# A fourth pair by seven products in eight groups of each feed-forward, with the joins, transposes and first loads re-ordered

## The chip, the core and the metric

The kernel runs on one core of a Trainium2 chip. The metric is the device time of one execution in microseconds (us), lower is better. Before the change it is 2086.14 us, the median of three runs (2083.84 to 2087.06). The core has a matrix engine (TensorE, PE in the profile, with its weight loads as PEld), a vector engine (VectorE, DVE), a scalar engine (ScalarE, ACT), GpSimd (POOL) and SyncE (SP), which issues most of the DMAs. Each engine executes its instructions in the order in which the program issues them. TensorE alone writes PSUM, the accumulator memory, in banks of 512 columns; everything else is in SBUF.

## What is computed

A Conformer block on x of 256 rows by 2048 features: a feed-forward, a mixer (convolution and gated units), cross-attention into a memory, a second feed-forward and a last norm. The change lies in the two feed-forwards:

```python
def swiglu_ffn(h, w_in, w_out):            # w_in 2048 x 11264, w_out 5632 x 2048
    gate, up = jnp.split(h @ w_in, 2, axis=-1)
    return (jax.nn.silu(gate) * up) @ w_out

h = rms_norm(x, ffn1_norm[l])
x = x + MACARON_SCALE * swiglu_ffn(h, ffn1_w_in[l], ffn1_w_out[l])
...
h = rms_norm(x, ffn2_norm[l])
x = x + MACARON_SCALE * swiglu_ffn(h, ffn2_w_in[l], ffn2_w_out[l])
```

All is float32. Each operand is split into a high part in the matrix engine's float32r format and the rest, and a product is three matmuls: high by high, high by low, low by high.

## The kernel before

**Groups.** A feed-forward takes the hidden width of 5632 in 11 groups of 512 (`NG`, counted from 0). A group multiplies 256 tokens by 1024 columns (512 of gate, 512 of up) over 2048 features, that is 16 weights of 128 x 1024. After the groups come two blocks of the second product, 44 weights each.

**Pairs.** Group 0 takes its 16 weights plainly: 12 matmuls of 512 columns for each (`by_two`, two token halves by two column halves by three, L358 to L361). In groups 1 to 10 the weights go in 8 pairs, by a pattern of letters. A pair with C is taken plainly, 24 matmuls. A pair with S is taken as a 2 x 2 product with seven products instead of eight (`seven`, L345 to L347): 21 matmuls, for which sums of weight halves (L628, L629, L632, L635) and sums of x (`sides`) are made first. The seven products stand in accumulators "5", "7", "6", "1" and, with the plain ones, in "2", "3", "4", "8". The pattern is `SCSCSCCC`: three pairs by seven.

**Joins.** After the second of the four items of a group's last pair by seven, "5", "7", "6" and "1" are complete: `joins_sevens` copies "1" (ScalarE, L694) and makes the common sums (VectorE, L695 to L698). After the group's last item `joins_eights` adds "2", "3", "4", "8" (L702), and `give` applies silu, scale and product (L712, L714) and transposes the group's result in 32 x 32 blocks on VectorE (L717, 128 x 1024). The result leaves to DRAM (`leaves`, SP) behind the third item of the next group; it comes back later (`back`) and `turn` splits it into the operand of the second product. Six accumulators come from one pool (`ps`) and two ("6", "7") from another (`pa`), so a group's banks become those of the next.

**A weight's way.** An item of the line (`Item`, `Line`) is a weight or a part of one: it is loaded by SP into one of eight raw buffers, ScalarE casts it to the high part (L451), VectorE subtracts (L428) and so makes the low part, TensorE uses it. `Line.produce` issues casts ahead of use as far as places for the parts are free (nine) and `most` allows; the subtraction of an item is issued after the cast of the next. In each group some weights are summed instead (`SUMMED`, by number 0 to 15): ScalarE writes the negated high part and the high part (L566, L567), and an accumulating DMA of GpSimd (L568) adds the weight from DRAM; VectorE does nothing for them. Two buffers (hl_s and half of `more`) serve these in turn; each is filled anew after its use. In the groups with three pairs by seven, weights 2, 7 and 13 are summed.

**Operands.** In a group x (`x_hl`) is the stationary operand and the weight's parts the moving one. The weight's places are three of `hl`, two of `ring`, two of `hl_l`, one of `hl_h` and one of `more`; in the second product also `hl_out` and `more_out`, with `hl_s`, `hA`, `hB`, `hC` as stationary operands.

**Where tiles lie.** Pools lie one behind the other in a partition in the order in which they are opened, and a tile takes a multiple of 32 bytes. By the laid-out program, tiles of `const`, `big`, `wraw`, `whl` and `ev` (x_hl, ring, hA, hB, more_out, raw, hl) start at a multiple of 64 bytes. The small tiles of `st` follow. What lies behind them, the pools `xt`, `own`, `low` and later ones (more, raws_out, hl_s, h, z, hl_out, sums, hl_l, hC), starts at 32 modulo 64. `hl_h` is laid from the upper end and starts at 32 modulo 64 too. A tile of 8 floats, `to_64` (L97), stands in `st` already.

**The start.** Group 0 of the first feed-forward loads x by columns (`xT`, two at a time) beside its weights, and x by rows in four quarters of 512 KB, whose squares (L894) give the root `r_x` that `give` needs. All are on SP's queue in the order of the weights: the quarters stand in front of weights 2, 4, 6 and 8, the squares behind weights 2, 4, 6 and 8.

Of the kernel before, what the change touches and what calls it, by code (L numbers as in the profile page):

```python
# [33 lines left out]
SCALE = float(HD) ** -0.5  # L34


PATTERNS = (["SCSCSCCC"] * 11, ["SCSCSCCC"] * 11)


SUMMED = tuple([()] + [(7, 13)] + [(2, 7, 13)] * 8 + [(2, 7)] for _ in range(2))  # L40

OUT_S = ((9, 11, 13, 15, 17, 19), (9, 11, 13, 15, 17, 19))
# [37 lines left out]
def layer(ctx: ExitStack, tc: tile.TileContext, a: dict):  # L82
# [299 lines left out]
    class Item:  # L382

        def __init__(self, use=None, loads=(), held=None, keys=(), pre=None, src=None, n=1024, frees=(), post=(), make=None):
            self.use, self.loads, self.held, self.keys, self.pre, self.src = use, loads, held, keys, pre, src
            self.n, self.frees, self.post, self.make = n, frees, list(post), make
            self.place = self.hl = None

    class Line:

# [73 lines left out]
        def run(self):  # L464
            traced = nc.cur_bb.bb.instructions
            begin = len(traced)
            self.fetch()
            self.produce()
            for s, item in enumerate(self.items):
                assert self.made > s, (s, len(self.places), len(self.raws), item.missing)  # L470
                if self.ahead is item:
                    self.subtract()
                if item.use is not None:
                    item.use(item.hl)
                if item.place is not None:
                    self.places.append(item.place)
                self.used = s + 1
                self.produce()
                for part in item.post:
                    part()  # L480
            last = {}
            for i in traced[begin:]:
                if i.engine in last:
                    tc.add_manual_dep(
                        i, last[i.engine].name,
                        mybir.DependencyInfo(mybir.DependencyClass.NoSync, mybir.DependencyReason.DATA),
                        reason="line",
                    )
                last[i.engine] = i

    class FeedForward:
# [6 lines left out]
        def __init__(self, stack, tags, name, x_hl, gain, w_in, w_out, patterns, sums, steps, out_s):  # L498
# [37 lines left out]
            self.in_spare = self.fixed(raws)  # L536
            self.line.places.extend(self.in_ring + self.in_low + self.in_high)
            self.line.raws.extend([Place(lambda: wraw.tile([P, 1024], F32, name="raw")) for _ in range(4)] + self.in_spare)

        def fixed(self, tiles):  # L540
            return [Place(lambda x=x: x) for x in tiles]
# [131 lines left out]
        def pairs(self, j, steps, kinds, b):  # L673
# [16 lines left out]
                    i += 1  # L690
            return out

        def joins_sevens(self, b, p1, u2, u4, u5):
            nc.scalar.copy(out=p1, in_=b["1"])  # L694
            nc.vector.tensor_tensor(out=u2, in0=p1, in1=b["6"], op=ALU.add)  # L695
            nc.vector.tensor_tensor(out=u4, in0=u2, in1=b["5"], op=ALU.add)
            nc.vector.tensor_tensor(out=u2, in0=u2, in1=b["7"], op=ALU.add)
            nc.vector.tensor_tensor(out=u5, in0=u2, in1=b["5"], op=ALU.add)  # L698

        def joins_eights(self, b, p1, u2, u4, u5):  # L700
            for acc, u in (("2", p1), ("3", u4), ("4", u2), ("8", u5)):
# [2 lines left out]
        def give(self, j, gates, ups):  # L704
            flat, r = self.stage[j % 2], self.r
            h = flat.rearrange("p (q t n) -> p q t n", q=4, t=2)

            def by_q(x):
                return x.rearrange("p (q n) -> p q n", q=4)

            for t in range(2):
                nc.scalar.activation(out=h[:, :, t], in_=by_q(gates[t]), func=AF.Silu, scale=r[:, t:t + 1])  # L712
            for t in range(2):
                nc.vector.scalar_tensor_tensor(  # L714
                    out=h[:, :, t], in0=by_q(ups[t]), scalar=r[:, t:t + 1], in1=h[:, :, t], op0=ALU.mult, op1=ALU.mult
                )
            nc.vector.transpose(out=flat, in_=flat)  # L717

        def leaves(self, j):
# [7 lines left out]

        def group(self, j):
            b = {"begun": set()}
            parts = self.pairs(j, range(len(self.patterns[j])), lambda p: self.patterns[j][p] == "S", b)  # L730
            p1, u2, u4, u5 = self.u
            self.last_seven[1].post.append(lambda: self.joins_sevens(b, p1, u2, u4, u5))
            parts[-1][-1].post += [
                lambda: self.joins_eights(b, p1, u2, u4, u5), lambda: self.give(j, (p1, u2), (u4, u5)),
            ]
            return parts

        def block(self, n, places, done):
            b = {"begun": set()}
            steps = self.steps[n]  # L740
            parts = self.pairs(NG + n, steps[0], lambda p: p in steps[1], b)
            made = []

            def join():
                made.append(places())
                self.joins_sevens(b, *made[0])

            self.last_seven[1].post.append(join)
            if done is not None:
                parts[-1][-1].post.append(lambda: (self.joins_eights(b, *made[0]), done(made[0])))  # L750
            return parts, b, made

        def begin(self, before, after, scales):
            acc = []

            def use(k):
                def go(w):
                    if k == 0:
                        acc.extend(token_accs())
                    first = [(t, g) for t in range(2) for g in range(2)] if k == 0 else []  # L760
                    by_two(acc, self.x_hl[:, k], w[:, 0], w[:, 1], k, first, k == KD - 1)
                return go

            items = []
            for k in range(KD):
                held = {}
                items.append(Item(
                    use(k), [(0, self.w_in[0, :, k], None)], held, src=lambda held=held: held[0][0], frees=(0,),
                    post=after.get(k, []),
                ))  # L770
                items[-1].pre = lambda k=k: before(k)
            for i in range(len(self.spairs)):
                for q, part in enumerate(self.sides(i)):
                    items[3 * i + q + 3].post.append(part)
            self.r, parts = scales
            parts = parts + [
                lambda: nc.scalar.activation(out=st.tile([P, 1], F32, name="warm"), in_=ones[:, 0:1], func=AF.Silu)
            ]
            for i, part in enumerate(parts):
                items[14 - len(parts) + i].post.append(part)  # L780
            items[13].post.append(lambda: self.summed_load(self.early))
            items[15].post += [
                lambda: self.give(0, [acc[t][0] for t in range(2)], [acc[t][1] for t in range(2)]),
                lambda: self.summed(self.early),
            ]
            self.ends = [KD]
            return items
# [71 lines left out]
    def groups(ff, items):  # L859


        for j in range(1, NG):
            parts = ff.group(j)
            flat = [item for part in parts for item in part]
            flat[2].post.append(lambda j=j: ff.leaves(j - 1))
            if j == 1:
                flat[4].post.append(lambda: ff.summed(1 - ff.early))
            if j == NG - 1:
                flat[1].post.append(lambda: (ff.back(0), ff.back(1)))
                flat[4].post.append(lambda: ff.back(2))  # L870
                for i, item in enumerate(flat[-6:]):
                    item.post.insert(0, ff.turn(i))
                ff.in_ring[0].until = ff.in_ring[1].until = len(items) + flat.index(ff.last_seven[-1])
            items += flat
# [5 lines left out]
    with ExitStack() as stack:  # L880
# [7 lines left out]
        def x_load(c):  # L888
            return lambda: nc.sync.dma_start(
                out=squares[c], in_=a["x"][c // 2 * P:(c // 2 + 1) * P, c % 2 * 1024:(c % 2 + 1) * 1024]  # L890
            )
# [10 lines left out]
        root[0] = both(  # L902
            lambda: nc.vector.tensor_tensor(out=r_x, in0=tot[:, 0], in1=tot[:, 1], op=ALU.add), root[0]
        )
        items = ff.begin(x_arrives, {2 * c + 2: [x_squares(c)] for c in range(4)}, (r_x, root))
        halves = [slice(G, 2 * G), slice(0, G)]

        def early_load():
# [8 lines left out]
        for k in range(1, KD):  # L917
            beside_load = []
            if k % 2 == 0:
                beside_load.append(lambda k=k: nc.sync.dma_start(out=xT[:, k:k + 2], in_=a["xT"][:, k:k + 2]))  # L920
            if k in (2, 4, 6, 8):
                beside_load.append(x_load(k // 2 - 1))
            if k == 11:
                beside_load.append(lambda: nc.sync.dma_start(out=pv, in_=a["pv"]))
            items[k].loads = [(0, a["ffn1_w_in"][0, :, k], both(*beside_load))]
# [43 lines left out]
        def more_out():  # L969
# [5 lines left out]
            ff.out_forms = [  # L975
                forms[:, q * 1024:(q + 1) * 1024].rearrange("p (f two n) -> p f two n", two=2, n=P) for q in range(6)
            ]
            ff.leaves(NG - 1)

        def hl_out():  # L980
            line.places.extend(ff.fixed([ff.own.tile([P, 2, 1024], F32R, name="hl_out", tag="z")]))
# [30 lines left out]
        flat = [item for part in parts for item in part]  # L1012
        for i in range(6, 2 * NG):
            flat[i - 6].post.append(ff.turn(i))
        flat[16].post.append(hl_out)
        items += flat
        ff.in_high[0].until = len(items) - 1
# [13 lines left out]
                flat.append(memory_squares((i - at - 3) // 2))  # L1031
        items += flat
        line.add(items)
        line.most = lambda s: 3 + s + max(0, s - 12)
        line.run()
        turns = turned(rest["o2"], 1)
        x_hl = rest["x_hl"]
# [397 lines left out]
    with ExitStack() as stack:  # L1435
# [38 lines left out]
        groups(ff, items)  # L1474
        rest = {}
        sums = st.tile([P, 2, 4], F32, name="sums")
        most = [st.tile([P, 1], F32, name=f"f_most{t}") for t in range(2)]

        def quarters(o):
# [6 lines left out]
        def more_out():  # L1486
# [5 lines left out]
            ff.out_forms = [  # L1492
                forms[:, q * 1024:(q + 1) * 1024].rearrange("p (f two n) -> p f two n", two=2, n=P) for q in range(6)
            ]
            ff.leaves(NG - 1)

        def hl_out():
            line.places.extend(ff.fixed([ff.own.tile([P, 2, 1024], F32R, name="hl_out", tag="z")]))
# [85 lines left out]
        flat = [item for part in parts for item in part]  # L1584
        for i in range(6, 2 * NG):
            flat[i - 6].post.append(ff.turn(i))
        flat[16].post.append(hl_out)
        items += flat
        ff.in_high[0].until = len(items) - 1
# [40 lines left out]
        kept[-1].post.append(ending)  # L1630
        items += flat
        line.add(items)
        line.most = lambda s: 4 + s + s // 4
        line.run()


# [79 lines left out]
```

## Time and profile before

| | |
|---|---|
| median of three runs | 2086.14 us (2083.84 to 2087.06) |
| the profiled execution, time | 2084.38 us |
| its span, first to last instruction | 2082.6 us |
| granted TensorE clock | 0.999 of full speed |
| first feed-forward: TensorE's first weight, group 0's silu, group 1's silu | 5.8, 56.0, 99.2 us |
| second feed-forward: group 0's second silu, last group's silu | 1415.6, 1839.8 us |
| mean DMA rate over the span | 225 GB/s |

A row of the profile names the line of the kernel, the engine, the operation, out<-in by the program's names, the shapes, and a count. In the views by group there follow busy time, the mean length of one, and the idle time of the engine in front of them with what ended it. Matmuls overlap: the length of one is more than the distance to the next.

### The profile page before, as it was taken

To read this page: it belongs to the slowest core of one execution; us is meant where nothing else is said; L and a number is where in the kernel's file an instruction comes from. 1 tells how busy PE (TensorE), PEld (TensorE's weight loads), DVE (VectorE), ACT (ScalarE), POOL (GpSimd) and SP (SyncE) were. 2 spreads that over 40 slices of the span, in tenths; PEclk is the share of its full clock that TensorE was granted. 3 is DMA by queue.
4 is the path that set the end of the run, shared out by engine and by line. 5 is a ranking of instruction groups with operands and counts; after the bars stand their busy time and mean duration, and the time that the engine had idled before them with its cause. 6 is when DMAs were issued, how large, how long until landed. Compare 5 with 4: busy or idle time off the path is not lost.

```text
span 2082.6 us, 26581 instructions
## 1 busy us (share of the span) xinstructions
PE 2068.9 (99%) x9544; PEld 1713.2 (82%) x9544; DVE 1703.4 (82%) x2358; ACT 1197.7 (58%) x1514; POOL 62.8 (3%) x81
## 2 busy tenths in 40 slices
PE   9999999999999999999999999999999999999998
PEld 7788888888888888888888899888888888888886
DVE  7998888878987789989887666788888888789875
ACT  7666556646555654444665455566565556565454
POOL 0000000000000000000000000000000000000002
PEclk9999999999999999999999999999999999999999
DMA  8888777869656576656555543678788778797574
GB/s 337 282 249 274 255 232 237 270 181 296 204 197 237 196 238 200 190 178 186 175 192 199 185 160 119 201 296 274 235 254 272 241 225 254 217 260 246 175 215 166
DMA packets 139525, 468.57 MB, mean 225 GB/s; under 512 B 15488, under 2 KB 27136, under 8 KB 138752
## 3 DMA queue, kind: packets, MB, share of 16 engines
q1 hardware_dynamic: 130464, 434.35, 61.2%
q0 software_dynamic: 8352, 31.46, 8.0%
q8 instruction: 75, 1.23, 0.2%
q10 hardware_dynamic: 576, 1.06, 0.1%
q14 instruction: 58, 0.48, 0.1%
HBM read 451.08 MB, written 15.73 MB: 224 GB/s over the span
## 4 chain that ended last, share of the span: by engine, by line
PE 93%; DVE 2%; DMA 1%; ACT 1%; issue 0%; POOL 0%; DVEq 0%; ACTq 0%; SPq 0%
PE acc L359 15%; PE acc L358 15%; PE acc L361 15%; PE acc L158 8%; PE acc L208 5%; PE acc L209 5%; PE acc L207 5%; PE acc L345 5%; PE acc L346 5%; PE acc L347 5%; PE acc L166 4%; PE aux L345 2%; PE aux L346 2%; PE aux L347 2%; DMA raw<-in_memT 1%; DVE hl L129 0%
## 5 line engine op out<-in xcount | busy, mean ns | idle before, releaser
L128 ACT CAST hl<-raw 128x1024 fp32r<-128x1024 f32 (+1 forms) x228 | 235.6, 1035 | 224.6 <-PE acc L209 92.8
L129 DVE TENSOR_TENSOR hl<-raw,hl 128x1024 fp32r<-128x1024 f32 (+1 forms) x228 | 273.9, 1203 | 95.6 <-ACT hl L128 94.5
L451 ACT CAST hl<-raw 128x1024 fp32r<-128x1024 f32 (+1 forms) x136 | 134.3, 1000 | 94.6 <-PE acc L361 38.1
L428 DVE TENSOR_TENSOR hl<-raw,hl 128x1024 fp32r<-128x1024 f32 (+1 forms) x136 | 156.6, 1156 | 26.8 <-ACT hl L451 25.1
L208 PE MATMUL acc<-hl,x_hl 128*128 128x512 f32 x256 | 100.7, 393 | 0.2 <-DVE hl L129 0.2
L208 PE MATMUL acc<-hl,m_hl 128*128 128x512 f32 x256 | 100.3, 392 | 0.0
L209 PE MATMUL acc<-hl,m_hl 128*128 128x512 f32 x256 | 100.3, 392 | 0.0
L209 PE MATMUL acc<-hl,x_hl 128*128 128x512 f32 x256 | 99.9, 390 | 0.0
L359 PE MATMUL acc<-hl,x_hl 128*128 128x512 f32 x248 | 97.0, 391 | 2.6 <-DVE hl L428 2.6
L358 PE MATMUL acc<-hl,x_hl 128*128 128x512 f32 x248 | 97.1, 392 | 0.0
L207 PE MATMUL acc<-hl,m_hl 128*128 128x512 f32 x256 | 90.9, 392 | 0.0
L207 PE MATMUL acc<-hl,x_hl 128*128 128x512 f32 x256 | 90.3, 392 | 0.0
L361 PE MATMUL acc<-hl,x_hl 128*128 128x512 f32 x248 | 76.4, 389 | 0.0
L451 ACT CAST hl<-raws_out 128x1024 fp32r<-128x1024 f32 (+1 forms) x53 | 51.0, 968 | 43.9 <-PE acc L361 22.3
L451 ACT CAST hl<-spare 128x1024 fp32r<-128x1024 f32 (+1 forms) x52 | 49.4, 968 | 34.9 <-DVE spare L635 18.0
L428 DVE TENSOR_TENSOR hl<-raws_out,hl 128x1024 fp32r<-128x1024 f32 (+1 forms) x53 | 59.1, 1121 | 10.5 <-ACT hl L451 9.3
L428 DVE TENSOR_TENSOR hl<-spare,hl 128x1024 fp32r<-128x1024 f32 (+1 forms) x52 | 57.4, 1116 | 12.1 <-ACT hl L451 11.4
L451 ACT CAST hl<-sums 128x1024 fp32r<-128x1024 f32 x34 | 35.7, 1049 | 54.4 <-DVE sums L629 53.8
L359 PE MATMUL acc<-hl_l,x_hl 128*128 128x512 f32 x168 | 66.5, 396 | 0.0
L359 PE MATMUL acc<-more,x_hl 128*128 128x512 f32 x168 | 66.5, 396 | 0.0
L358 PE MATMUL acc<-more,x_hl 128*128 128x512 f32 x168 | 66.5, 396 | 0.0
L358 PE MATMUL acc<-hl_l,x_hl 128*128 128x512 f32 x168 | 66.4, 395 | 0.0
(608 smaller groups left out, 5933.1 us busy)
## 6 DMA issues: line engine op xcount, KB each, us to landing
spare<-in_ffn_w_in SPq DMA_DIRECT2D x200, 512.0 KB, 6.4
raw<-in_ffn_w_in SPq DMA_DIRECT2D x151, 512.0 KB, 6.5
raw<-in_ffn_w_out SPq DMA_DIRECT2D x96, 512.0 KB, 4.4
raws_out<-in_ffn_w_out SPq DMA_DIRECT2D x76, 512.0 KB, 4.9
raw<-in_w_mix_vg SPq DMA_DIRECT2D x32, 512.0 KB, 4.4
raw<-in_w_k SPq DMA_DIRECT2D x32, 512.0 KB, 3.6
raw<-in_w_v SPq DMA_DIRECT2D x32, 512.0 KB, 4.1
raw<-in_w_mix_out SPq DMA_DIRECT2D x32, 512.0 KB, 4.3
```

The lines of the kernel that those rows point to most:

```text
L128: nc.scalar.copy(out=hl[:, 0, :size], in_=raw[:, :size])
L129: newest[0] = nc.vector.tensor_tensor(out=hl[:, 1, :size], in0=raw[:, :size], in1=hl[:, 0, :size].bitcast(F32), op=ALU.subtract)
L158: done = nc.tensor.matmul(acc, lhsT=hi[:, k], rhs=xs[k], start=first and k == 0, stop=last and k == kk - 1, skip_group_check=True,)
L207: nc.tensor.matmul(acc[t], lhsT=x[:, 0, s], rhs=hi[:, k], start=k0 + k == 0, stop=False)
L208: nc.tensor.matmul(acc[t], lhsT=x[:, 0, s], rhs=lo[:, k], start=False, stop=False)
L209: nc.tensor.matmul(acc[t], lhsT=x[:, 1, s], rhs=hi[:, k], start=False, stop=k0 + k == nk - 1)
L345: nc.tensor.matmul(acc, lhsT=x[0], rhs=hi, start=first, stop=False)
L358: nc.tensor.matmul(acc[t][g], lhsT=x[:, 0, s], rhs=hi[:, cols[g]], start=(t, g) in first, stop=False)
L359: nc.tensor.matmul(acc[t][g], lhsT=x[:, 0, s], rhs=lo[:, cols[g]], start=False, stop=False)
L361: done = nc.tensor.matmul(acc[t][g], lhsT=x[:, 1, s], rhs=hi[:, cols[g]], start=False, stop=last)
L428: nc.vector.tensor_tensor(out=hl[:, 1, :n], in0=item.raw[:, :n], in1=hl[:, 0, :n].bitcast(F32), op=ALU.subtract)
L451: nc.scalar.copy(out=item.hl[:, 0, :item.n], in_=item.raw[:, :item.n])
```

## The change

- `PATTERNS`: groups 2 to 9 of each feed-forward take `SCSCSCSC`, four pairs by seven; groups 1 and 10 keep `SCSCSCCC`. The x side of a fourth pair (6) is made in group 0 by `sides`.
- `SUMMED`: in groups 2 to 9 weights 2, 6, 11 and 15 are summed, in place of 2, 7 and 13.
- `ORDERS`: group 1 takes its pairs in the order 0, 2, 1, 3, and so on. `pairs`, which is not changed, takes two pairs by seven at the head together: the first two items of each, then the last two of each.
- `joins_first`: the copy of "1" is issued right behind the item's matmuls (`now`), in front of the casts that `produce` issues; the sums stay behind them. "5" + "7" is summed in another order with as many operations.
- `by_blocks`: the transpose is taken out of `give` and issued behind the second item of the next group; `leaves` goes behind the fourth item. For group 10 both go into the first block.
- `AHEAD`: `most` is 7 items past the end of the current group (6 for group 0, 9 for group 10), in group 0 also 4 and 6 items past the current one; before, it was 3 + s + max(0, s - 12) and 4 + s + s // 4 for item s.
- `to_64_too`: a second small tile of 8 floats in `st`.
- The quarters of x by rows stand in front of weights 4, 6, 8 and 10, their squares behind weights 6, 8, 10 and 11; the parts of the root behind 12, 13 and 14, and silu's table is loaded right behind the root.
- The first six turns stand three items earlier in group 10.

```diff
-PATTERNS = (["SCSCSCCC"] * 11, ["SCSCSCCC"] * 11)
+PATTERNS = (["SCSCSCCC"]*2 + ["SCSCSCSC"]*8 + ["SCSCSCCC"],)*2
+ORDERS = {1: (0, 2, 1, 3, 4, 5, 6, 7)}
-SUMMED = tuple([()] + [(7, 13)] + [(2, 7, 13)] * 8 + [(2, 7)] for _ in range(2))
+SUMMED = tuple([()] + [(7, 13)] + [(2, 6, 11, 15)] * 8 + [(2, 7)] for _ in range(2))
+AHEAD = tuple((h, [e, 7, 7, 7, 7, 7, 7, 7, 7, 7, 9]) for h, e in ((4, 6), (6, 6)))
...
                 if item.use is not None:
                     item.use(item.hl)
+                for part in item.now:
+                    part()
...
+        def ahead(self, rules):
+            head, more = rules
+            def most(s):
+                for j, end in enumerate(self.ends):
+                    if s <= end:
+                        return min(end + more[j], s + head if j == 0 else 1 << 30)
+                return 1 << 30
+            return most
...
+        def joins_first(self, b, p1):
+            nc.scalar.copy(out=p1, in_=b["1"])
         def joins_sevens(self, b, p1, u2, u4, u5):
-            nc.scalar.copy(out=p1, in_=b["1"])
             nc.vector.tensor_tensor(out=u2, in0=p1, in1=b["6"], op=ALU.add)
             nc.vector.tensor_tensor(out=u4, in0=u2, in1=b["5"], op=ALU.add)
+            nc.vector.tensor_tensor(out=u5, in0=u4, in1=b["7"], op=ALU.add)
             nc.vector.tensor_tensor(out=u2, in0=u2, in1=b["7"], op=ALU.add)
-            nc.vector.tensor_tensor(out=u5, in0=u2, in1=b["5"], op=ALU.add)
...
+        def by_blocks(self, j):
+            flat = self.stage[j % 2]
             nc.vector.transpose(out=flat, in_=flat)
...
-            parts = self.pairs(j, range(len(self.patterns[j])), lambda p: self.patterns[j][p] == "S", b)
+            parts = self.pairs(j, ORDERS.get(j, range(8)), lambda p: self.patterns[j][p] == "S", b)
+            self.last_seven[1].now.append(lambda: self.joins_first(b, p1))
             self.last_seven[1].post.append(lambda: self.joins_sevens(b, p1, u2, u4, u5))
...
-            flat[2].post.append(lambda j=j: ff.leaves(j - 1))
+            flat[1].post.append(lambda j=j: ff.by_blocks(j - 1))
+            flat[3].post.append(lambda j=j: ff.leaves(j - 1))
-                for i, item in enumerate(flat[-6:]):
+                for i, item in enumerate(flat[-9:-3]):
...
-        items = ff.begin(x_arrives, {2 * c + 2: [x_squares(c)] for c in range(4)}, (r_x, root))
+        items = ff.begin(x_arrives, {(6, 8, 10, 11)[c]: [x_squares(c)] for c in range(4)}, (r_x, root))
-            if k in (2, 4, 6, 8):
-                beside_load.append(x_load(k // 2 - 1))
+            if k in (4, 6, 8, 10):
+                beside_load.append(x_load(k // 2 - 2))
...
-        line.most = lambda s: 3 + s + max(0, s - 12)
+        line.most = ff.ahead(AHEAD[0])
...
+        st.tile([P, 8], F32, name="to_64_too")
...
-        line.most = lambda s: 4 + s + s // 4
+        line.most = ff.ahead(AHEAD[1])
```

More of the change, by code (lines that the diff above doesn't have):

```diff
@@ L387, in __init__ @@
             self.place = self.hl = None
+            self.now = []
     class Line:
@@ L742, in block, with first @@
             made = []
-            def join():
+            def first():
                 made.append(places())
-                self.joins_sevens(b, *made[0])
-            self.last_seven[1].post.append(join)
+                self.joins_first(b, made[0][0])
+            self.last_seven[1].now.append(first)
+            self.last_seven[1].post.append(lambda: self.joins_sevens(b, *made[0]))
             if done is not None:
@@ L775, in begin @@
             self.r, parts = scales
[L776 to L780, printed above, removed]
+            silu = lambda: nc.scalar.activation(out=st.tile([P, 1], F32, name="warm"), in_=ones[:, 0:1], func=AF.Silu)
+            for i, part in enumerate([parts[0], lambda: (parts[1](), silu()), parts[2]]):
+                items[12 + i].post.append(part)
             items[13].post.append(lambda: self.summed_load(self.early))
@@ L977, in more_out @@
             ]
-            ff.leaves(NG - 1)
         def hl_out():
@@ L1014, in layer @@
             flat[i - 6].post.append(ff.turn(i))
+        flat[1].post.append(lambda: ff.by_blocks(NG - 1))
+        flat[2].post.append(lambda: ff.leaves(NG - 1))
         flat[16].post.append(hl_out)
@@ L1494, in more_out @@
             ]
-            ff.leaves(NG - 1)
         def hl_out():
@@ L1586, in layer @@
             flat[i - 6].post.append(ff.turn(i))
+        flat[1].post.append(lambda: ff.by_blocks(NG - 1))
+        flat[2].post.append(lambda: ff.leaves(NG - 1))
         flat[16].post.append(hl_out)
```

## The prediction

> **What bounds the kernel now.** I read the page first, for the busy shares, then the list of what TensorE waited for, then stretches of one group each, and only then single matmuls in the timeline.
>
> ```profile
> span 2082.6 us, 26581 instructions
> ...
> PE 2068.9 (99%) x9544; PEld 1713.2 (82%) x9544; DVE 1703.4 (82%) x2358; ACT 1197.7 (58%) x1514; POOL 62.8 (3%) x81
> ...
> GB/s 337 282 249 274 255 232 237 270 181 296 204 197 237 196 238 200 190 178 186 175 192 199 185 160 119 201 296 274 235 254 272 241 225 254 217 260 246 175 215 166
> ```
>
> TensorE (PE) is busy for all but 13.7 us. A busy share can hide stalls, so the second view is the list of its waits (who, for whom; total us, times, longest):
>
> ```profile
> PE acc L359 <- DVE hl L428: 2.6, 2, 1.4
> ...
> PE acc L345 <- ACT h L712: 0.4, 1, 0.4
> ```
>
> Three waits inside the feed-forwards, 3.0 us together. So the time is the number of matmuls times the distance from one to the next, and two things can shorten it: fewer matmuls, or a smaller distance. The third view gives both; it adds up eight stretches of 42.00 us, one per group, in the second feed-forward:
>
> ```profile
> sum 336.00, PE 336.00 PEld 273.60 DVE 286.44 ACT 203.16 POOL 20.04; mean PE 42.00 PEld 34.20 DVE 35.81 ACT 25.39 POOL 2.50
> ```
>
> A group of three pairs by seven is 3 x 21 + 5 x 24 = 183 matmuls, so one takes 42.0 / 183 = 0.229 us (they overlap; the 390 ns of a matmul's own row isn't its price). VectorE (DVE) has 35.8 us of work in the same 42.0 and is the next bound.
>
> **The seventh product.** Eight groups of each feed-forward turn one more pair from 24 matmuls to 21: 16 x 3 = 48 matmuls. At 0.227 us (the clean distance, next part) that is **10.9 us** off TensorE.
>
> **The filler.** It is 32 bytes a partition at the end of the small pool. What lies behind it now starts at 32 modulo 64 and will start at 0; hl_h, laid from the other end, stays at 32. The timeline (start, length) shows that it matters:
>
> ```profile
> 125.12 0.40 PE L358 MATMUL acc<-hl_h,x_hl 128*128 128x512 f32 x1
> ...
> 127.92 0.40 PE L358 MATMUL acc<-hl,x_hl 128*128 128x512 f32 x1
> ...
> 130.64 0.40 PE L358 MATMUL acc<-hl_s,x_hl 128*128 128x512 f32 x1
> ```
>
> Each row begins a weight of 12 matmuls. With hl_h streaming (offset 32) it lasts 127.92 - 125.12 = 2.80 us, with hl (offset 0) 130.64 - 127.92 = 2.72 us: 233 against 227 ns a matmul. The view by tile (count: shortest/median/longest ns) shows which pairs are slow:
>
> ```profile
> L359 PE MATMUL acc<-hl_s,x_hl x112: 392/396/397, 72.4 to 1802.4; 128*128 128x512 f32 x112
> ...
> L359 PE MATMUL acc<-hl,hl_s x48: 391/396/397, 479.6 to 1973.1; 128*128 128x512 f32 x48
> ...
> L359 PE MATMUL acc<-hl_h,hl_s x8: 389/389/393, 476.8 to 1839.7; 128*128 128x512 f32 x8
> ...
> L361 PE MATMUL acc<-more_out,hl_s x8: 393/395/397, 613.7 to 1976.4; 128*128 128x512 f32 x8
> ```
>
> Slow (396) is a moving operand at 32 with a stationary one at 0, and the reverse; both at 32 (hl_h with hl_s) is fast (389). So it is the difference of the two offsets, not a slow place in the memory. Pairs that differ and will not: 2,442 matmuls in 63 groups, of which the largest is
>
> ```profile
> L358 PE MATMUL acc<-hl_l,x_hl 128*128 128x512 f32 x168 | 66.4, 395 | 0.0
> ```
>
> and the smallest the x8 row of more_out with hl_s above. At 6 to 7 ns each that is 14.7 to 17.1 us; the 48 matmuls of hl_h with hl_s and hC go the other way and take back 0.3. I take **15 us**; the bounds are 0 (offsets don't cause it) and 17.
>
> The Trainium skill speaks against this term: "TensorE: Matmul & The Clock Gate", Part 2, step 1, says that the streaming operand and the weight load have SBUF read ports of their own, so that a load takes nothing from a running matmul. By that rule the filler is worth nothing; the rows above, 396 against 389 by the pair, don't agree with it.
>
> **The start.** PE loses 1.4 us twice, on the second and third weight. The third:
>
> ```profile
> 15.01 0.50 PE L359 MATMUL acc<-hl,x_hl 128*128 128x512 f32 x1 [1.39 <-DVE hl L428]
> ```
>
> and on ScalarE its cast:
>
> ```profile
> 11.84 1.05 ACT L451 CAST hl<-raw 128x1024 fp32r<-128x1024 f32 x1 [2.94 <-DMA raw<-in_ffn_w_in]
> ```
>
> That cast waited for a weight which came behind the first quarter of the x rows on SP's queue. 0.52 MB at the page's first 337 GB/s is 1.56 us; with the x rows two weights on, the weight lands that much earlier and the wait of 1.4 goes. The second weight's wait stays: its subtraction is queued on DVE behind the next x column, whose load isn't moved. The order 0, 2, 1 in group 1 lets four items pass before banks 2, 3, 4, 8 are wanted, so the wait on L712 goes (0.6 with the slow first matmul). Together **2.1 us**. Nothing is late next there: the x rows now end at weight 11, which moves the root by two or three items (5 to 8 us). Before it was
>
> ```profile
> 46.01 0.16 DVE L271 RECIPROCAL r_x<-rt 128x2 f32<-128x2 f32 x1
> ```
>
> and the first use of r_x is the second row of L712's view, at 56.0:
>
> ```profile
> L712 ACT ACTIVATE h<-acc,r_x x4: 676/682/692, 56.0 to 1415.6; 128x512 f32<-128x512 f32 x4
> ```
>
> Two or three microseconds are left; if that cover is gone, group 1's banks are late by as much, once in each feed-forward.
>
> **What VectorE pays.** A pair by seven needs four sums of 512 (L628 to L635), three subtractions of 1024 and one of 512. Two plain weights need two of 1024, less those that are summed by the DMA. Plain weights that DVE subtracts go from 10 - 3 = 7 to 8 - 4 = 4 a group, so the 1024s come out even (16 and 16) and five operations of 512 are added. Their price back to back is that of the four joins, in DVE's timeline:
>
> ```profile
> 222.89 2.47 DVE L702 TENSOR_TENSOR spare<-spare,acc 128x512 f32<-128x512 f32 x4
> ```
>
> 0.61 each, so + 3.0: 35.8 becomes **38.8 us**. TensorE's group becomes 42.0 - 0.7 - 0.5 (80 slow matmuls a group x 6.2 ns) = **40.8 us**. DVE may then stand idle 2.0 us a group instead of 6.2. What it waits for now, in two groups (181.6 to 265.9):
>
> ```profile
> DVE ring L428 <- ACT ring L451: 5.5, 2, 2.7
> DVE hl_l L428 <- ACT hl_l L451: 2.3, 2, 1.2
> DVE spare L695 <- ACT spare L694: 1.3, 2, 0.7
> DVE hl L428 <- ACT hl L451: 0.8, 3, 0.3
> DVE sums L629 <- DMA spare<-in_ffn_w_in: 0.8, 1, 0.8
> DVE sums L629 <- DMA raw<-in_ffn_w_in: 0.8, 1, 0.8
> DVE hl_h L428 <- ACT hl_h L451: 0.3, 1, 0.3
> ```
>
> The first row is DVE being ahead: the cast waits for TensorE to free a buffer. It goes when DVE has less time. The third is the joins waiting for the copy of p1 (L694); issued in front of the casts, the copy no longer stands behind one (1.05), and the casts behind it lose only its 0.6. The rest is 5.0 / 2 = 2.5 us a group: more than 2.0. If all of it stayed, 0.5 us x 16 = 8 us would come back; with the p1 wait too, 1.2 x 16 = 18; if DVE's present 6.2 of idle stayed whole, 4.2 x 16 = 67; at the other end 0. The nearest rows are the stretches of the first groups (length, then busy times; the last two are groups 1 and 10, counted from 0):
>
> ```profile
> 16.00:56.00 40.00, 40.00 (x175) 32.68 (x174) 34.35 (x57) 33.59 (x51) 0.00 (x0) 1.00 0.88 338
> 56.00:98.00 42.00, 41.64 (x181) 33.58 (x180) 37.65 (x44) 29.44 (x34) 3.64 (x4) 1.00 0.91 288
> ...
> 434.00:480.00 46.00, 46.00 (x201) 37.55 (x200) 33.76 (x43) 22.06 (x27) 0.00 (x0) 1.00 0.68 210
> ```
>
> Group 1 has DVE at 37.65 of 42.0, with the DMA at 0.91, and TensorE lost 0.36. So waits shrink when time is short. I take 0.25 us a group, **4 us** back.
>
> **What costs nothing, and its cover.** Four weights a group summed instead of three: ScalarE gets two passes for one, with the extra pair + 2.7 on 25.4 of 40.8, under 70%. The accumulating DMA (L568) starts after the first of them and from its issue on lands in
>
> ```profile
> DMA to landing us min/median/max: 5.1/6.9/9.9
> ```
>
> With about 1 us of pass in front that is 6 to 11 us; from one use of a buffer to the next it serves, 15 us are left (weight 11 ends 10 us before its group does, weight 2 of the next begins 4.8 after; 24 before the change). Beyond that TensorE would wait. The transpose, 1.25 on DVE, moves behind the second item of the next group: the joins' banks come free by as much earlier for whatever is behind, and on SP the store still stands two items behind it. The fourth pair's sides add four sums of 128 columns and a subtraction of 512 on DVE in group 0, under 2 us where 34.35 of 40.0 are used (the first row). The turns three items earlier lie in group 10, where DVE has 12 us idle. The limit of seven past a group's end keeps casts off the queues in front of the joins; its price is DVE idling there, which is in the 4 us.
>
> **Sum.** The profiled execution took 2084.38 (2082.6 of span and 1.8 around it): - 10.9 - 15.0 - 2.1 + 4.0 = 2060.4. It lies 1.8 under the median of the runs, 2086.14; I say **2061**, for itself 2054 to 2067.
>
> **Rivals.**
> - DVE becomes the bound: 9 to 18 us come back instead of 4, 2066 to 2076, say 2072. For it: 2.5 us of waits against 2.0 of room. Against it: group 1's row.
> - The filler is worth nothing (the page's rule above): 2061 + 15 = 2076. For it: no tile behind the small pool lies at 0 now, so distance and offset can't be told apart fully. Against it: the x8 row of two offset tiles at 389.
> - Slower: the waits on casts and DMA are of the order of the instructions and stay whole, DVE holds TensorE in each of the 16 groups. It decides from 28 / 16 = 1.75 us a group, that is when 3.7 of today's 6.2 us of idle stay; whole, 2057 + 67 = 2124. Group 1's row speaks against it.
> - The parts cancel, within 4 us of 2086 (some 1.5 us a group come back).
>
> **Chances.** Forecast 0.62, DVE the bound 0.17, filler worth nothing 0.10, cancelled 0.05, slower 0.06. The range, 2053 to 2077, takes the first three but for their ends. 0.2% (4 us) is about what a measurement of this kernel can tell from no change: faster 0.89, same 0.05, slower 0.06.
>
> **What would show it.** Matmuls of hl_l, more, hl_s, hC at 389, hl_h still at 396; 48 records fewer; groups of about 40.8 us; DVE near 38.8 in each; no wait at 56.8 and one wait less at the start. Wrong would be: TensorE waiting for DVE's subtractions or for a bank at the start of groups 2 to 9, DVE busy with hardly a wait while TensorE idles, or hl_l still at 396.

## The result, and the profile after

The changed kernel takes 2058.61 us (median of four runs, 2057.98 to 2059.55) against 2086.19 (now a median of four runs too): a ratio of 0.987 with a 95% interval of 0.9853 to 0.9887, 1.3% faster. The forecast was 2061 with 2053 to 2077. The profiled execution took 2058.24 us (before: 2084.38), its span 2056.3.

The kernel after has its lines further down: L345 to L347 of the kernel before are L351 to L353, L358, L359 and L361 are L364, L365 and L367, L428 is L435, L451 is L458, L702 is L724, L712 is L734 and L714 is L736. The page of the kernel after, its first two lines of figures:

```profile
span 2056.3 us, 26663 instructions
...
PE 2040.6 (99%) x9496; PEld 1703.3 (83%) x9496; DVE 1752.2 (85%) x2448; ACT 1233.2 (60%) x1568; POOL 77.3 (4%) x97
```

9544 - 9496 = 48 matmuls are gone, as forecast, TensorE is still busy throughout, and VectorE has 49 us more to do. The view by tile (count: shortest/median/longest ns), first for hl_s, then for hl_h, says what became of the distance:

```profile
L365 PE MATMUL acc<-hl_s,x_hl x144: 388/389/398, 73.6 to 1778.9; 128*128 128x512 f32 x144
...
L365 PE MATMUL acc<-hl,hl_s x48: 388/389/398, 469.6 to 1947.9; 128*128 128x512 f32 x48
```

```profile
L365 PE MATMUL acc<-hl_h,x_hl x72: 392/396/398, 26.6 to 1804.9; 128*128 128x512 f32 x72
```

Both of hl_s's pairs went from 396 to 389; hl_h, which did not move, stayed at 396. The stretch of one group with four pairs by seven (length, then busy times of PE, PEld, DVE, ACT, POOL, the clock, the DMA's share and GB/s):

```profile
178.00:219.00 41.00, 41.00 (x182) 33.84 (x182) 38.76 (x49) 27.61 (x31) 3.49 (x4) 1.00 0.88 269
```

VectorE at 38.76 is what the prediction had worked out (38.8). But the list of TensorE's waits didn't get shorter:

```profile
PE aux L352 <- DVE ring L435: 1.6, 1, 1.6
PE acc L352 <- DVE hl L435: 1.3, 1, 1.3
PE aux L242 <- DVE ones L239: 1.1, 1, 1.1
PE acc L365 <- DVE hl L435: 0.9, 1, 0.9
PE acc L352 <- DVE ring L435: 0.4, 1, 0.4
```

The three waits under L352 (1.6, 1.3 and 0.4) are new. They all stand in group 1 of the first feed-forward. The timeline has two of them:

```profile
55.52 0.50 PE L352 MATMUL acc<-hl,ring 128*128 128x512 f32 x1 [1.32 <-DVE hl L435]
...
58.76 0.50 PE L352 MATMUL aux<-ring 128*128 128x512 f32 x1 [1.58 <-DVE ring L435]
```

To see where the 26.3 us of the span went, the matmuls of each trace were counted off and the time taken from a group's first matmul to that of the next (us):

```
                                          before    after   difference
start to first weight                       5.77     5.36     - 0.4
first feed-forward   group 0               47.73    45.72     - 2.0
                     group 1               42.87    46.24     + 3.4
                     groups 2 to 9        338.07   327.64    - 10.4
                     group 10              42.16    41.61     - 0.5
its second product, mixer, attention      894.52   892.06     - 2.5
second feed-forward  groups 0 and 1        86.67    85.88     - 0.8
                     groups 2 to 9        337.72   327.64    - 10.1
                     group 10              42.16    41.61     - 0.5
second product and the end                244.94   242.53     - 2.4
```

Groups 2 to 9 carry 20.5 of it, the second products, the middle and the other groups the rest, and the start, which was to gain, has given 1.0 back by the end of group 1. The table also shows that a group before took 42.2 us (337.72 / 8): the 42.00 in the prediction is the length of the stretches that it looked at, not of a group.

### The profile page after: what moved, and what is told of

Its sections match the earlier page's. It is cut to its first block, busy times and chain, and to the rows that moved or that the text cites. A ratio compares the mean times of both kernels' runs of the same rounds, so it can differ in the third digit from the quotient of the medians.

```text
span 2056.3 us, 26663 instructions
## 1 busy us (share of the span) xinstructions
PE 2040.6 (99%) x9496; PEld 1703.3 (83%) x9496; DVE 1752.2 (85%) x2448; ACT 1233.2 (60%) x1568; POOL 77.3 (4%) x97
## 4 chain that ended last, share of the span: by engine, by line
PE 93%; DMA 2%; DVE 2%; ACT 2%; issue 1%; SPq 0%; POOL 0%; ACTq 0%; DVEq 0%
PE acc L365 14%; PE acc L364 14%; PE acc L367 14%; PE acc L164 9%; PE acc L352 5%; PE acc L351 5%; PE acc L353 5%; PE acc L214 5%; PE acc L215 5%; PE acc L213 5%; PE acc L172 4%; PE aux L352 2%; PE aux L351 2%; PE aux L353 2%; DMA raw<-in_ffn_w_in 1%
## 5 line engine op out<-in xcount | busy, mean ns | idle before, releaser
L458 ACT CAST hl<-raw 128x1024 fp32r<-128x1024 f32 (+1 forms) x138 | 136.9, 1001 | 92.6 <-PE acc L367 36.7
L435 DVE TENSOR_TENSOR hl<-raw,hl 128x1024 fp32r<-128x1024 f32 (+1 forms) x138 | 159.4, 1159 | 25.2 <-ACT hl L458 22.9
L214 PE MATMUL acc<-hl,x_hl 128*128 128x512 f32 x256 | 100.8, 394 | 0.3 <-DVE hl L135 0.3
L215 PE MATMUL acc<-hl,x_hl 128*128 128x512 f32 x256 | 99.9, 390 | 0.0
L213 PE MATMUL acc<-hl,x_hl 128*128 128x512 f32 x256 | 90.3, 392 | 0.0
L458 ACT CAST hl<-raws_out 128x1024 fp32r<-128x1024 f32 (+1 forms) x51 | 49.1, 967 | 46.6 <-PE acc L367 26.9
L365 PE MATMUL acc<-hl,x_hl 128*128 128x512 f32 x192 | 75.1, 391 | 1.2 <-DVE hl L435 0.9
L364 PE MATMUL acc<-hl,x_hl 128*128 128x512 f32 x192 | 75.0, 391 | 0.2 <-ACT hl L142 0.2
L458 ACT CAST hl<-sums 128x1024 fp32r<-128x1024 f32 x42 | 44.2, 1052 | 51.7 <-DVE sums L649 50.6
L365 PE MATMUL acc<-more,x_hl 128*128 128x512 f32 x184 | 71.7, 390 | 0.0
L364 PE MATMUL acc<-more,x_hl 128*128 128x512 f32 x184 | 71.6, 389 | 0.0
L588 POOL DMA_DIRECT2D hl_s<-in_ffn_w_in x36 | 31.5, 875 | 1059.6 <-ACT hl_s L586 1059.6
L435 DVE TENSOR_TENSOR hl<-raws_out,hl 128x1024 fp32r<-128x1024 f32 (+1 forms) x51 | 56.6, 1116 | 13.7 <-ACT hl L458 12.6
L586 ACT ACTIVATE more<-spare 128x1024 fp32r<-128x1024 f32 x36 | 38.1, 1058 | 45.4 <-PE acc L365 45.4
L164 PE MATMUL acc<-o_hl,hl 128*128 128x512 f32 x256 | 62.8, 392 | 0.0
L164 PE MATMUL acc<-x_hl,hl 128*128 128x512 f32 x256 | 61.9, 392 | 0.0
L164 PE MATMUL acc<-y_hl,hl 128*128 128x512 f32 x256 | 61.8, 391 | 0.0
```

Source lines behind the costliest of these rows:

```text
L164: done = nc.tensor.matmul(acc, lhsT=hi[:, k], rhs=xs[k], start=first and k == 0, stop=last and k == kk - 1, skip_group_check=True,)
L213: nc.tensor.matmul(acc[t], lhsT=x[:, 0, s], rhs=hi[:, k], start=k0 + k == 0, stop=False)
L214: nc.tensor.matmul(acc[t], lhsT=x[:, 0, s], rhs=lo[:, k], start=False, stop=False)
L215: nc.tensor.matmul(acc[t], lhsT=x[:, 1, s], rhs=hi[:, k], start=False, stop=k0 + k == nk - 1)
L364: nc.tensor.matmul(acc[t][g], lhsT=x[:, 0, s], rhs=hi[:, cols[g]], start=(t, g) in first, stop=False)
L365: nc.tensor.matmul(acc[t][g], lhsT=x[:, 0, s], rhs=lo[:, cols[g]], start=False, stop=False)
```

## The experiments

All times are medians beside runs of the kernel before on the same chip; where a few us matter, the stretches are counted as in the table.

**The filler, from both sides.** In the first run the kernel after loses its second small tile, in the second the kernel before gets it as its only edit.

```diff
-        st.tile([P, 8], F32, name="to_64_too")
```

> The kernel after without its second small tile. Theory A (the offset of the two operands to 64 bytes sets the distance of matmuls): the tiles behind the small pool are at 32 modulo 64 again, matmuls with hl_l, more or hl_s against x_hl go from 389 back to 396 ns, hl_h with hl_s back to 389, and the time rises by about 15 us, from 2058.6 to 2073. Rival B (the filler does nothing, the shorter rows of after come from something else in the change): 2058 to 2060 and rows that stay at 389.

> The kernel before with the second small tile as its only edit. Theory A: the rows of hl_l, more, hl_s and hC go from 396 to 389, those of hl_h with hl_s from 389 to 396, and the time falls by about 15 us, from 2086.2 to 2071; the waits of the start stay as they are. Rival B: 2086 within 2 us.

Measured: 2075.36 without it (+ 16.8) and 2069.87 with it alone (- 16.3; ratio to before 0.9923, 0.9908 to 0.9938). The view by tile of the first,

```profile
L365 PE MATMUL acc<-hl_s,x_hl x144: 395/396/397, 73.8 to 1792.7; 128*128 128x512 f32 x144
...
L365 PE MATMUL acc<-hl_h,hl_s x8: 389/392/398, 472.8 to 1830.0; 128*128 128x512 f32 x8
```

and of the second:

```profile
L359 PE MATMUL acc<-hl_s,x_hl x112: 389/389/393, 72.0 to 1789.7; 128*128 128x512 f32 x112
...
L359 PE MATMUL acc<-hl_h,hl_s x8: 393/397/398, 472.8 to 1826.7; 128*128 128x512 f32 x8
```

Thirty-two bytes move the two rows in opposite ways, hl_s with x_hl down and hl_h with hl_s up. So where the operands start sets the distance, and the filler is 16 to 17 us of the 27.6. The rival "worth nothing" falls. The Trainium skill ("TensorE: Matmul & The Clock Gate", Part 2, step 1) gives the streaming operand and the weight load an SBUF read port each, so that a load takes no read bandwidth from the running matmul; that a filler is then worth nothing was the prediction's own step, and these rows don't agree with it. Whether it is the load that costs the 6 ns, they don't say.

**The seventh product alone.** The kernel after with three pairs by seven everywhere:

```diff
-PATTERNS = (["SCSCSCCC"]*2 + ["SCSCSCSC"]*8 + ["SCSCSCCC"],)*2
+PATTERNS = (["SCSCSCCC"] * 11, ["SCSCSCCC"] * 11)
-... [(2, 6, 11, 15)] * 8 ...
+... [(2, 7, 13)] * 8 ...
```

> The kernel after with three pairs by seven in every group and weights 2, 7 and 13 summed, all else as in after; group 0 then makes the x sides of three pairs, not of four. Groups 2 to 9 should take 40.9 + 3 x 0.227 = 41.6 us, + 10.9 us over both feed-forwards. For the start of the first feed-forward (first matmul to the end of group 1, 97.3 us with what lies ahead of it in after, 95.7 in the kernel before with the filler): theory E (VectorE's work in group 0 is the bound, and the fourth pair's sides, some 1.8 us, are what is too much): 94 to 95.5 us, in all 2066 to 2067. Rival D (the late root and its two table loads): 97 us, in all 2069.

Measured: 2067.47, + 8.9. Groups 2 to 9 take 333.09 us in either feed-forward against 327.64: 10.9 us, the forecast term to the tenth. The start to the end of group 1 takes 95.5 us against 97.3, so the three pairs win 1.8 us back there. Over the whole span the fourth pair is worth 10.1 us (2066.4 against 2056.3).

**How near VectorE is to the bound.** One more weight a group goes through VectorE:

```diff
-SUMMED = ... [(2, 6, 11, 15)] * 8 ...
+SUMMED = ... [(2, 6, 11)] * 8 ...
```

> The kernel after with weight 15 subtracted on VectorE again in groups 2 to 9 (weights 2, 6 and 11 are summed): 1.2 us of VectorE more in each, 40.0 of 40.9. It asks how near the bound VectorE is. If its waits shrink when time is short (the prediction's step), groups 2 to 9 stay at 40.9 to 41.1 us and the time at 2058 to 2062. If the 2.0 us of room were all used by waits that stay, each group grows by about 1.2 us and the time by up to 19 us, to 2077.

Measured: 2062.96, + 4.4. In the first feed-forward groups 2 to 7 stay at 40.9 to 41.1 us and groups 8 and 9 take 41.6; the second does the same from group 7 on. VectorE falls behind a little in each group and the places made ahead pay for it until they are used up. The stretch of group 8 and TensorE's only wait from there to the end of group 10:

```profile
343.60:385.20 41.60, 41.22 (x182) 33.72 (x180) 39.84 (x49) 26.78 (x30) 2.63 (x3) 1.00 0.79 253
```

```profile
PE acc L351 <- DVE spare L724: 1.1, 3, 0.4
```

L724 are the sums of `joins_eights`: TensorE waits for a bank at the start of a group, and with the two late matmuls behind each wait the three cost 1.9 us. So with 39.84 us of work VectorE's own pace is 41.6 us a group; without the extra subtraction (1.14 from its start to the next) it is, as an estimate, some 40.5, half a microsecond inside TensorE's 40.95. The kernel after hides its extra VectorE work with little to spare.

**The limit on casts ahead.** The two old rules put back:

```diff
-        line.most = ff.ahead(AHEAD[0])
+        line.most = lambda s: 3 + s + max(0, s - 12)
-        line.most = ff.ahead(AHEAD[1])
+        line.most = lambda s: 4 + s + s // 4
```

> The kernel after with the two old rules for how far casts may run ahead. If the limit past a group's end matters, the joins come behind casts that wait for a buffer, and TensorE waits for a bank at the start of groups: 0.3 us or more in each of 16, 2063 or more. If it does not, 2058 to 2060, and group 1 of the first feed-forward shows whether the narrow limit in group 0 has a part in its 46.2 us: if so it falls to 44 or less.

Measured: 2059.4, no difference. Group 1 of the first feed-forward falls from 46.2 to 45.0, group 2 rises from 40.9 to 42.5, and groups 3 to 10 keep their times to the hundredth. The expected 0.3 a group was wrong: from group 3 on the limit isn't needed at this load. What it does is to keep group 2 from waiting for the joins of group 1 (1.3 us for L724 without it), and the end of group 2 comes 0.7 us earlier with it; the span is the same.

**The start.** Four runs ask why group 1 got slower. The order of group 1 off:

```diff
-ORDERS = {1: (0, 2, 1, 3, 4, 5, 6, 7)}
+ORDERS = {}
```

> The kernel after with group 1's pairs in the plain order 0, 1, 2, 3. Theory C (two pairs by seven in a row ask VectorE for 13 us of work in 9.5 us of TensorE, so it falls behind in group 1): group 1 of the first feed-forward shrinks from 46.2 to 42 or 43 us, the waits of 1.3 and 1.6 us on VectorE's subtractions go, a wait of at most 1 us on the banks comes back, and the time is 2 to 4 us lower, 2055 to 2057. Rival D (the root and its two table loads, moved to the end of group 0, hold ScalarE and so VectorE up): the waits stay and the time stays at 2058 to 2059.

Measured: 2059.25, group 1 at 46.7 and its end at 98.3. Theory C falls. The two waits are exchanged for others, the largest of which is the one the new order was to take away:

```profile
PE acc L351 <- ACT h L734: 1.3, 1, 1.3
```

The old start, with the fourth pair's sides kept:

```diff
-... {(6, 8, 10, 11)[c]: [x_squares(c)] for c in range(4)}
+... {2 * c + 2: [x_squares(c)] for c in range(4)}
-            if k in (4, 6, 8, 10):
-                beside_load.append(x_load(k // 2 - 2))
+            if k in (2, 4, 6, 8):
+                beside_load.append(x_load(k // 2 - 1))
-            for i, part in enumerate([parts[0], lambda: (parts[1](), silu()), parts[2]]):
-                items[12 + i].post.append(part)
+            for i, part in enumerate([*parts, silu]):
+                items[10 + i].post.append(part)
```

> The kernel after with the x rows in front of weights 2, 4, 6 and 8 again, their squares and the root at the places of before and silu's table loaded one item behind the root's end; group 1 keeps its new order. The wait of 1.4 us on the third weight comes back by both theories. Theory C: group 1 of the first feed-forward stays at 45 to 47 us, so the time rises by 1.5 to 2 us to 2060 or 2061. Rival D: group 1 falls to 42 or 43 us and the time falls by 1 to 3 us in all, to 2056 or 2057.

Measured: 2057.43. Group 1 falls to 43.8, near what rival D had, but group 0 rises from 45.7 to 48.0: start to the end of group 1 is 97.0 against 97.3. What is lost ahead is saved behind. To tell the root's place from that, the x rows were moved and the root kept early:

```diff
-... {(6, 8, 10, 11)[c]: [x_squares(c)] for c in range(4)}
+... {(5, 6, 7, 9)[c]: [x_squares(c)] for c in range(4)}
-            if k in (4, 6, 8, 10):
-                beside_load.append(x_load(k // 2 - 2))
+            if k in (4, 5, 6, 8):
+                beside_load.append(x_load((4, 5, 6, 8).index(k)))
-            for i, part in enumerate([parts[0], lambda: (parts[1](), silu()), parts[2]]):
-                items[12 + i].post.append(part)
+            for i, part in enumerate([*parts, silu]):
+                items[10 + i].post.append(part)
```

> The kernel after with the x rows in front of weights 4, 5, 6 and 8, their squares behind weights 5, 6, 7 and 9, and the root and silu's table at the places of before (behind items 10 to 13). Rival D (the late root and two table loads in a row): the third weight's wait stays away and group 1 falls to 43.8 us or less as in the run with the old start; first matmul to the end of group 1 takes 95 us with what lies ahead of it, in all 2056. Theory E (VectorE's work in group 0 is the bound; an earlier start of TensorE is given back): 96.5 to 97.3, in all 2058.

Measured: 2059.86, 97.6 to the end of group 1, group 1 at 46.5. Rival D falls too. Whatever TensorE gains on the first weights, it waits for in group 1, because what it needs there is made by VectorE and ScalarE, who aren't earlier: VectorE comes to the product of group 0's result (L736) at 56.2 us in the kernel after, at 55.8 with the order off and with the old start and at 56.5 in this run, but at 54.4 with three pairs by seven. The kernel after, both stretches (group 0, then group 1):

```profile
5.40:51.10 45.70, 44.55 (x193) 35.99 (x194) 35.99 (x60) 35.84 (x57) 0.00 (x0) 1.00 0.96 367
51.10:97.30 46.20, 42.89 (x184) 34.03 (x183) 40.20 (x52) 32.04 (x37) 3.63 (x4) 1.00 0.82 270
```

VectorE has 40.2 us of work in group 1, and in group 0, beside 36.0, it waits 8.6 us for ScalarE's x columns (L313) while the DMA is at 0.96. On ScalarE these columns stand behind casts, and the casts wait for weights from the DMA (6.6 us); for a column's own load ScalarE waited 0.3. Two edits shortened the stretch by more than half a microsecond and kept the gain through group 2, those that take the fourth pair's sides out of group 0: the run with three pairs by seven above, and the next but one. (The old limits on casts gained 0.9 and lost it again in group 2.)

**hl_h as well, and later sides.** hl_h gets a tile of 8 floats beside it, and in the second and third run the fourth pair's sides are summed and split in group 1, which doesn't use them:

```diff
             highs = [high.tile([P, 2, 1024], F32R, name="hl_h")]
+            high.tile([P, 8], F32, name="to_64_right")
...
                 for q, part in enumerate(self.sides(i)):
-                    items[3 * i + q + 3].post.append(part)
+                    if i == 3 and q > 0:
+                        self.late_sides.append(part)
+                    else:
+                        items[3 * i + q + 3].post.append(part)
...
                 flat[4].post.append(lambda: ff.summed(1 - ff.early))
+                for q, part in enumerate(ff.late_sides):
+                    flat[8 + q].post.append(part)
```

> The kernel after with hl_h too at a multiple of 64 bytes: a tile of 8 floats stands beside it. Theory A (the difference of the offsets): the 552 matmuls with hl_h go from 396 to 389 ns, by 6.5 to 7 ns each, 3.7 us off, 2055. If the place at the upper end were slow in itself: 2058 to 2059, rows that stay at 396.

> As the run with hl_h at 64, and the fourth pair's sides, which group 2 is the first to use, are summed and split behind items 9 and 10 of group 1; only their scaling by ScalarE stays in group 0. Theory E (VectorE's work up to the first items of group 1 is too much): up to 1.8 us off the stretch from the start to the end of group 1, 2053. If the weights' arrival is what holds group 0 up, the stretch stays at 97 us but for hl_h's share, 2055.

The third has no order of group 1 either:

```diff
-ORDERS = {1: (0, 2, 1, 3, 4, 5, 6, 7)}
+ORDERS = {}
```

> As the run with the late sides, and group 1 with its pairs in the plain order. The order off alone changed the stretch to the end of group 1 by + 0.9 us. Theory E: VectorE is less behind, the same change is worth between - 1 and + 1 us, 2052 to 2054.

Measured: 2059.54, 2055.06 and 2056.54. The first missed: hl_h is at a multiple of 64 and its rows hardly moved (below). The late sides brought the stretch to the end of group 1 from 97.2 to 95.6 us, 1.6 of the 1.8 that theory E had. The plain order on top is worth nothing in that stretch (95.5).

**hl_h at 128.** With 24 floats beside hl_h in place of 8:

```diff
-            high.tile([P, 8], F32, name="to_64_right")
+            high.tile([P, 24], F32, name="to_128_right")
```

> As the run with the late sides, but with 24 floats beside hl_h in place of 8: it starts at a multiple of 128 bytes, where x_hl, hA, hB, hC and the other places start, and not only of 64. Theory G (the two operands' offsets to 128 bytes have to agree): the rows of hl_h go from 394 to 389 ns, 552 matmuls by 6 ns, 3.4 us off, 2051.5. Theory H (the upper end of the memory is slow in itself, or 64 bytes are what counts and something else slows hl_h): rows stay at 394, 2055.

Measured: 2055.61, and hl_h still slow. Theory G falls, as far as it goes by 128 bytes. The view by tile of hl_h, of the run at 64 and then of the run at 128:

```profile
L364 PE MATMUL acc<-hl_h,x_hl x72: 394/394/394, 26.2 to 1805.0; 128*128 128x512 f32 x72
L365 PE MATMUL acc<-hl_h,x_hl x72: 394/394/394, 26.5 to 1805.2; 128*128 128x512 f32 x72
```

```profile
L364 PE MATMUL acc<-hl_h,x_hl x72: 395/398/398, 26.6 to 1802.6; 128*128 128x512 f32 x72
L365 PE MATMUL acc<-hl_h,x_hl x72: 387/392/392, 26.8 to 1802.8; 128*128 128x512 f32 x72
```

The pattern of single matmuls changes with the place, the mean doesn't: 12 matmuls with hl_h last 2.80 us in the run at 64 (from 26.24 to 29.04 in the timeline) and 2.79 in the run at 128 (26.59 to 29.38), against 2.72 with hl.

All three versions with the late sides have medians under both kernels': 2055.06, the lowest, is a ratio to before of 0.9852 (0.9836 to 0.9869), 3.5 us under the changed kernel's median, though the kernel before was lower too beside it (2085.34). Of that, 1.7 us show in the traces (a span of 2054.9 against 2056.6 for the same kernel without the late sides); the rest is no more than runs differ by.

## Why the prediction was right

By its own steps, with what was measured in place of each:

- **The seventh product, - 10.9.** Right: 10.9, by the run with three pairs.
- **The filler, - 15.** Right in kind and a little small: 15.6 by the spans of before with and without it, 16.3 by the medians, 16.8 taken out of after. Its price by the difference of pairs held (hl_s with x_hl down, hl_h with hl_s up). Its reason, offsets modulo 64, did not: hl_h at a multiple of 64 and of 128 is still slow. That 32 bytes were enough was luck: they took the tiles from 480 to 0 modulo 512, not only to a multiple of 64.
- **The start, - 2.1.** Wrong. From the start to the end of group 1 it was 96.4 us before and is 97.3; before with the filler alone has 95.7. The wait on the third weight did go (group 0 is 2.0 shorter), but the sentence that failed is "Nothing is late next there". VectorE's and ScalarE's part for group 1 was, and group 1 grew by 3.4. Another sentence failed with it, under what costs nothing: the fourth pair's sides "under 2 us where 34.35 of 40.0 are used". That idle time was no cover, since VectorE spends most of it waiting for x columns that ScalarE converts behind casts of weights still on their way. The sides cost 1.6 to 1.8 us, by two runs. The x rows' two microseconds were given back whichever way the root was placed; which of ScalarE's chain and the DMA's 0.96 sets the rest, the runs leave open. Up to the end of group 2 the loss is not there: the kernel before with the filler waits for the joins of group 1 at the head of group 2, which takes 43.8 us,

```profile
PE acc L345 <- DVE spare L702: 1.9, 1, 1.9
```

  and ends group 2 at 139.5 us (138.8 with three matmuls fewer). The kernel after, whose group 2 takes 40.9, ends it at 138.2: some 0.6 us won where 2.1 were forecast.
- **What VectorE pays, + 4.** Too much: groups 2 to 9 take 40.95 us on the average (327.64 / 8) in either feed-forward, and TensorE waits for nothing in them. That is 0.15 over the 40.8 that had been worked out with no wait at all, but the 40.8 started from 42.0; from the 42.2 that a group took, the same working gives 41.0. So nothing of the 4 us came back in these groups. Of VectorE's waits in three of these groups

```profile
DVE h L736 <- ACT h L734: 1.4, 3, 0.5
DVE hl L435 <- ACT hl L458: 1.2, 3, 0.7
DVE hl_l L435 <- ACT hl_l L458: 1.2, 3, 0.7
DVE ring L435 <- ACT ring L458: 0.9, 2, 0.7
DVE hl_h L435 <- ACT hl_h L458: 0.3, 1, 0.3
```

  none is for a DMA or for the copy of p1, and they sum to 1.7 us a group where 2.5 to 3.2 had been feared. That is the claim that waits shrink when time is short. The run with three summed weights shows how close it was: 1.14 us more, and the room is gone.
- **The sum.** - 24.0 was forecast and - 26.1 measured between the profiled executions. Four spans split it: 2082.6 before, 2067.0 with the filler (- 15.6), 2066.4 with everything but the fourth pair (- 0.6), 2056.3 after (- 10.1, that is 10.9 less some 0.8 that came back outside groups 2 to 9). By the medians the steps are 16.3, 2.4 and 8.9, so a single step is known to a microsecond or two. The start gained about 1.5 less than forecast, the sides had stood at nothing, VectorE's 4 weren't needed, and the filler gave a little more: the total is nearer than its terms.
- **The rivals.** DVE as the bound in every group and the slower case ask for more than 1.7 us of waits a group that stay; there were none that TensorE felt. The upper price of the first, 1.2 x 16, is 19 and not 18, which changes nothing. Accumulating DMAs, one more a group, landed in time (5.3 to 10.0 us after their issue, and TensorE waited for none). The limit on casts, which stood in the 4 us, cost and gave nothing over the whole.

## What to carry to other kernels

When TensorE is busy throughout, look at the distance between matmuls pair by pair of operands: a few nanoseconds on a quarter of the matmuls were worth more here than dropping a product. An engine's idle time is cover only if the work can be done in it: ask what each of its waits is for before giving it more; and a gain on the first transfers is a gain only if what the later stage needs becomes earlier too. Whether the next bound is near is tested by adding one operation per stage, and by looking at late stages, since buffers made ahead hide a small deficit for several of them.

## What the runs showed of the hardware that was not expected

A matmul of 512 columns costs 227 ns with some pairs of operands and 233 with others, and neither 64 nor 128 bytes is the rule. In the program's layout the tiles that pair well agree in their start modulo 512: all but hl_h at 0 in the kernel after, and hl_h with hl_s, both at 480, in the kernel before. Slow against tiles at 0 were starts at 480 (before and after), 448 (2.80 us for 12 matmuls) and 384 (2.79). So all pairs seen fit "the two starts agree modulo 256 or 512"; 448 and 384 against 0, which agree modulo 64 and modulo 128, rule these two out. hl_h at a multiple of 512 was not tried, so for hl_h its place at the upper end isn't excluded, though its rows of 389 with hl_s before speak against that; hl_s, hl_l, more and hC change between 396 and 389 with 32 bytes. The Trainium skill says in "SBUF — State Buffer", section "SBUF: two separate sides", that on the engines' side PE never waits on anyone; these rows don't tell what the 6 ns are a wait for, only that TensorE's two operands aren't indifferent to each other's place.
